# Score tiles in pairs, and the low rotary keys in four strips of 32 rows

## The chip, the cores and the metric

The kernel runs on one core of one Trainium2 chip. TensorE multiplies matrices into PSUM (eight banks of 512 fp32 per partition), VectorE, ScalarE and GpSimd work elementwise, SyncE (SP) issues DMAs. The metric is the time of one execution in device microseconds, lower is better; the median of two runs of the kernel before is 1232.89 us.

## The reference

A two-layer encoder trunk on 1024 tokens of width 1024. Layer 0 projects the normalised input once and feeds two parallel attention groups of eight heads each; layer 1 is windowed attention. The change touches group B of layer 0, multi-head latent attention, whose scores are the sum of a latent part and a rotary part:

```python
def mla_attention(q_lat, q_rope, c_kv, k_rope, w_uv):
    scale = (B_NOPE + B_ROPE) ** -0.5            # 64 + 32 dimensions a head
    def block(args):
        ql, qr = args
        sc = (jnp.einsum('bqhc,bsc->bhqs', ql, c_kv)
              + jnp.einsum('bqhr,bsr->bhqs', qr, k_rope)).astype(jnp.float32) * scale
        p = jax.nn.softmax(sc, axis=-1).astype(c_kv.dtype)
        return jnp.einsum('bhqs,bsc->bqhc', p, c_kv)
    ...
```

The rotary key `k_rope` has 32 dimensions and is shared by all heads; each head has its own 32 rotary query dimensions.

## The kernel before, in words

All large products run in fp32r, and most operands are split into a high part (the value rounded to fp32r) and a low part (the rest), so that a product is the sum of high x high, high x low and low x high.

Layer 0's attention is 32 groups, one for each head and half of the queries: first 16 of group A (names a00 to a71), then 16 of group B (b00 to b71). A group has four score tiles, each of 128 queries by 1024 keys, that is two PSUM banks. For each tile `softmax_unit` (line 1057) issues the score matmuls of the two halves of 512 keys, then a negated row maximum on VectorE (`nm`), the exponential with its row sum on ScalarE (reads PSUM, writes the SBUF tile `P`, `Pa` or `Pb` in the profile), a reciprocal on VectorE (`rs`), and the scaling of `P` on GpSimd. `pv_step` (line 1076) then takes one block of 128 keys: four transposes of `P` into one PSUM bank, a high copy on ScalarE and a low difference on VectorE (`hla`, `hlb`), and two matmuls with the values (`VA`, `VB`) that add into one bank. `run_groups` (line 1097) records, for each group, the eight `pv_step`s of the group before and the four score tiles of this one, the tiles with the priority of the first or second step (`S_AT`).

In group B one half of a score tile is three matmuls with 128 rows (`qk_of`, lines 1343 to 1351): `q1` with `k1` (the latent high keys, and the high rotary key under both the high and the low rotary query), `q2` with `k2` (the latent cross terms), and `q1` with `krl`. `krl` is a 128 x 1024 tile that is zero except for rows 64 to 95, where it holds the low part of the rotary key; those rows meet the high rotary query in rows 64 to 95 of `q1`. It is made once in `b_krope` (line 1218). `b_heads` (line 1310) makes `q1`, `q2`, `k2` for two heads at a time and fetches the rotary rows of `q1` from DRAM (`qr_sp`) by DMAs that GpSimd issues.

The order of the work isn't the order of the program. A `Recorder` (line 106) collects every operation with its tiles, and a list scheduler (`run`) plays them through with a cost for each (`cost`, line 211), eight PSUM banks, 49 SBUF buffers of 4 KB a partition and a window of 400 operations; an operation starts when its engine is free, its inputs are ready and its tiles find room, lowest priority number first. Each engine's queue is then issued in the order so found. All engine instructions carry line 461, where the recorded calls are issued; the tile names tell them apart. An operation made under `issue_after(m)` isn't placed before `m` has started.

Of the kernel before, what the change touches and what calls it, by code (L numbers as in the profile page):

```python
# [19 lines left out]
P = 128  # L20
# [85 lines left out]
class Recorder:  # L106
# [104 lines left out]
    def cost(self, eng, method, regs, kw):  # L211
        n = max(r[4] for r in regs if r[1])
        ps = any(isinstance(r[0], VP) for r in regs)
        nin = max([r[4] for r in regs if not r[1]] or [n])
        if eng == "PE":
            if method == "transpose":
                return 109, 0
            lhs = [r for r in regs if r[0] is kw.get("lhsT")][0]
            c = max(lhs[4] / 1.2, n / 2.4) + 2.5
            if "float32r" not in str(lhs[6].dtype):  # L220
                c = max(426, 4 * n / 2.4 + 3)
            return c, 0
        if eng == "SP":
            return 70, 0
        if method == "dma_start":
            return 1050, 0
        m = max(n, nin)
        if eng == "DVE":
            if method == "reciprocal":
                return 70 + 6.4 * n, 0  # L230
            npt = sum(1 for r in regs if not r[1] and r[4] == 1 and m > 1)
            if method == "tensor_copy":
                return 64 + 1.04 * m if ps else 70 + 0.52 * m, 0
            if method in ("tensor_scalar", "tensor_scalar_mul"):
                return 60 * npt + (67 + 1.04 * m if ps else 70 + 0.52 * m), 0
            return 67 + 1.043 * m + 60 * npt, 0
        if eng == "ACT":
            return (53 if ps else 95) + 0.83 * m + (93 if "bias" in kw or not isinstance(kw.get("scale", 1.0), float) else 0) + (
                93 if "accum_out" in kw else 0), 0
        if method == "tensor_tensor":  # L240
            return (150 + 180 * n, 0) if "pow" in str(kw.get("op")) else (147 + 2.11 * n, 0)
        return 250 + 0.83 * n, 0
# [241 lines left out]
def encoder_kernel(ctx: ExitStack, tc: tile.TileContext, xt, ada_t, w_c1, w_c2, w_c3, w_g0, w_uq, w_ukv, w_out0, w_v1,  # L484
# [30 lines left out]
    def SM(name):  # L515
        return rec.tile(smp, [P, 16], F32, name, "sm")
# [28 lines left out]
    def f(ap):  # L545
        return ap.bitcast(F32)
# [507 lines left out]

    def softmax_unit(qk, name):
        S = PS(f"S{name}")
        first = None
        for b in range(2):  # L1060
            m_ = qk(S[:, b * 512:(b + 1) * 512], b)
            first = first or m_
        marks[name] = first
        nm = SM("nm")
        with rec.at(shift=PRIO["red"]):
            nc.vector.tensor_reduce(out=nm[:, 0:1], in_=S, axis=AX.X, op=ALU.max, negate=True)
        pt = U(f"P{name}")
        sm = SM("sm")
        with rec.at(shift=PRIO["exp"]):
            nc.scalar.activation(pt, S, AF.Exp, bias=nm[:, 0:1], accum_out=sm[:, 0:1])  # L1070
        r = SM("rs")
        nc.vector.reciprocal(r[:, 0:1], sm[:, 0:1])
        nc.gpsimd.tensor_scalar(pt, pt, r[:, 0:1], 1.0, op0=ALU.mult, op1=ALU.mult)
        return pt
# [22 lines left out]
    def run_groups(groups, before, after):  # L1097
        prev = None
        last = {}
        for n in range(len(groups) + 1):  # L1100
            g = groups[n] if n < len(groups) else None
            if g is not None:
                before(n)
                g["P"] = []
            acc = PV(f"pv{prev['name']}") if prev is not None else None
            at = {}
            if prev is not None:
                for kt in range(NT):
                    at[kt] = len(rec.ops)
                    last[n - 1, kt] = pv_step(prev["P"], prev["V"](kt), acc, kt, prev["name"])  # L1110
            if g is not None:
                for j in range(4):
                    with rec.at(at.get(S_AT[j])):
                        g["P"].append(softmax_unit(g["qk"](j), f"{g['name']}{j}"))
            if prev is not None:
                with rec.at(shift=PRIO["fin"]):
                    pv_final(acc, prev["og"](), prev["gate"](), prev["h"], prev["half"])
                prev["done"]()
            if g is not None:
                after(n)  # L1120
            prev = g
# [49 lines left out]
    for h in range(8):  # L1171
        for half in range(2):
            g = h // 4

            def qk_of(j, h=h, half=half, g=g):
                def qk(ps, b):
                    i = half * 4 + j
                    q = Qa[h][:, i * P:(i + 1) * P]
                    m_ = mm(ps, lhsT=q, rhs=khh[g][:, b * 512:(b + 1) * 512], start=True, stop=False)
                    mm(ps, lhsT=q, rhs=kll[g][:, b * 512:(b + 1) * 512], start=False, stop=True)  # L1180
                    return m_
                return qk

            groupsA.append(dict(
                name=f"a{h}{half}", h=h, half=half, qk=qk_of,
                V=lambda kt, g=g: VA[kt // 4][:, kt % 4, g, :, :].rearrange("p s d -> p (s d)"),
                og=lambda p=h // 2: og_get(("0", p)), gate=lambda p=h // 2: gT["0", p],
                done=(lambda p=h // 2: og_done(("0", p), p)) if h % 2 and half else (lambda: None)))
# [29 lines left out]
    def b_krope(mark):  # L1218
        ropeb = U("ropeb")
        load(ropeb[:, 0:512], tabs_d[:, 1024:1536], mark)  # L1220
        load(ropeb[:, 512:768], kr_sp, mark)
        krraw = ropeb[:, 512:768].rearrange("p (t c) -> p t c", t=8)
        rope["C"] = CTv = ropeb[:, 0:256].rearrange("p (t s e) -> p t s e", t=8, s=2)
        rope["S"] = STv = ropeb[:, 256:512].rearrange("p (t s e) -> p t s e", t=8, s=2)
        t = U("krt")
        t1 = t[:, 0:256].rearrange("p (t s e) -> p t s e", t=8, s=2)
        t2 = t[:, 256:512].rearrange("p (t s e) -> p t s e", t=8, s=2)
        z = t[:, 512:768].rearrange("p (t c) -> p t c", t=8)
        kr4 = krraw.rearrange("p t (s e) -> p t s e", s=2)
        nc.gpsimd.tensor_tensor(out=t1, in0=kr4, in1=CTv, op=ALU.mult)  # L1230
        for s in range(2):
            nc.vector.tensor_tensor(out=t2[:, :, s, :], in0=kr4[:, :, 1 - s, :], in1=STv[:, :, s, :], op=ALU.mult)
        nc.vector.tensor_tensor(out=z, in0=t[:, 0:256].rearrange("p (t c) -> p t c", t=8),
                                in1=t[:, 256:512].rearrange("p (t c) -> p t c", t=8), op=ALU.add)
        B["k1"] = [UR(f"k1{j}") for j in range(3)]

        B["krl"] = UR("krl")
        nc.gpsimd.memset(f(B["krl"]), 0.0)
        for half in range(2):
            pt = PT(f"krT{half}")  # L1240
            for j in range(4):
                nc.tensor.transpose(out=pt[0:32, j * P:(j + 1) * P], in_=z[:, half * 4 + j, :], identity=ident)
            c = slice(half * 512, half * 512 + 512)
            k1 = B["k1"][0]
            nc.scalar.copy(k1[64:96, c], pt[0:32, :])
            nc.scalar.copy(k1[96:128, c], pt[0:32, :])
            for other in B["k1"][1:]:
                hi_pool(other[64:128, c], f(k1[64:128, c]))
            sub(B["krl"][64:96, c], pt[0:32, :], f(B["k1"][0][64:96, c]))

    qr_sp = [dr.tile([256, 1024], F32, name=f"qr_sp{s}") for s in range(2)]

# [46 lines left out]
            nc.scalar.copy(vt[:, :, 0, :], v)  # L1299
            sub(vt[:, :, 1, :], v, f(vt[:, :, 0, :]))  # L1300

    q1, q2, k2 = {}, {}, {}

    def K2E(o, i):
        if K2_POOL:
# [4 lines left out]
    def b_heads(p, half):  # L1310
        e, o = 2 * p, 2 * p + 1
        for h in (e, o) if half == 0 else ():
            q1[h], q2[h], k2[h] = UR(f"q1{h}"), UR(f"q2{h}"), UR(f"k2{h}")
            nc.gpsimd.dma_start(out=q1[h][64:96, :], in_=qr_sp[0][h * 32:(h + 1) * 32, :])
            nc.gpsimd.dma_start(out=q1[h][96:128, :], in_=qr_sp[1][h * 32:(h + 1) * 32, :])
        c = slice(half * 512, half * 512 + 512)
        ps = PA(f"kn{p}{half}")
        L = [a[:, p * P:(p + 1) * P] for a in B["ukv"]]
# [22 lines left out]
    for h in range(8):  # L1341
        for half in range(2):
            def qk_of(j, h=h, half=half):
                def qk(ps, b):
                    i = slice((half * 4 + j) * P, (half * 4 + j + 1) * P)
                    s = slice(b * 512, (b + 1) * 512)
                    m_ = mm(ps, lhsT=q1[h][:, i], rhs=B["k1"][h % 3][:, s], start=True, stop=False)
                    mm(ps, lhsT=q2[h][:, i], rhs=k2[h][:, s], start=False, stop=False)
                    mm(ps, lhsT=q1[h][:, i], rhs=B["krl"][:, s], start=False, stop=True)
                    return m_  # L1350
                return qk

            groupsB.append(dict(
                name=f"b{h}{half}", h=h, half=half, qk=qk_of,
                V=lambda kt, h=h: VB[h // 4, kt // 2][:, kt % 2, h % 4, :, :].rearrange("p s d -> p (s d)"),
                og=lambda p=h // 2: og_get(("0", 4 + p)), gate=lambda p=h // 2: gT["0", 4 + p],
                done=(lambda p=h // 2: og_done(("0", 4 + p), 4 + p)) if h % 2 and half else (lambda: None)))
# [449 lines left out]
```

## Time and profile before

| | |
|---|---|
| median of two runs | 1232.89 us (1232.76 to 1233.02) |
| the profiled execution | 1230.13 us, span 1228.4 us |
| mean granted TensorE clock | 0.987 |
| matmuls with `krl` | 128, from 432.1 to 656.8 us |
| score tiles of group B | 64 (64 exponentials into `Pb`) |
| DMA | 106.72 MB, mean 87 GB/s |

The profile is one execution, seen by the hardware profiler. Rows in order of time begin with the start and the duration in us; rows by group end with the count, the busy time in us and the mean duration of one in ns, and behind the second bar the idle time of the engine before them, with what ended it. Rows of one tile give least, median and most in ns and the first and last start. The row of a window gives busy time and count for TensorE, its weight loads, VectorE, ScalarE and GpSimd, then the granted clock, the DMA share and GB/s. `128*128` is the part of the array (rows*columns) that an instruction uses. PE is TensorE, PEld its weight loads, DVE VectorE, ACT ScalarE, POOL GpSimd.

### The profile page before, as it was taken

What the parts mean: (1) busy time and instruction counts of PE and PEld (TensorE: products, weight loads), DVE (VectorE), ACT (ScalarE), POOL (GpSimd) and SP (SyncE); (2) the same over time, 40 slices, a digit from 0 to 9 for tenths busy, and PEclk for the clock granted to TensorE, in tenths of its full rate; (3) what the DMA queues carried; (4) which work ended last, traced back from release to release, by engine and by line L of the source; (5) the groups of instructions that cost most, each with busy time, mean ns of one, the idle gap of its engine ahead of it and who ended that gap; (6) DMA issues with size and microseconds to landing.
All of it is one profiled execution on the core that took longest, in us unless ns stands there. A gap on an engine that the chain in (4) does not pass through costs nothing.

```text
span 1228.4 us, 17931 instructions
## 1 busy us (share of the span) xinstructions
PE 1178.4 (96%) x6320; PEld 987.6 (80%) x6320; DVE 940.8 (77%) x1787; ACT 661.7 (54%) x1348; POOL 566.1 (46%) x551
## 2 busy tenths in 40 slices
PE   7999899999999999999999999899999999998997
PEld 6988788877877877888787888788888778876896
DVE  8977787887787888888889995759875687787243
ACT  4643366566655877787876221338654564653212
POOL 0069754445456545444358223406446354476321
PEclk9999899999999999999999999899999999999999
DMA  9601123131112210101054745000012111055112
GB/s 353 243 9 48 62 76 121 35 120 35 50 59 86 86 52 19 35 17 36 2 202 179 269 157 184 6 18 18 18 52 86 47 58 52 18 188 194 47 70 69
DMA packets 37338, 106.72 MB, mean 87 GB/s; under 512 B 3840, under 2 KB 9472, under 8 KB 37248
## 3 DMA queue, kind: packets, MB, share of 16 engines
q1 hardware_dynamic: 36480, 103.48, 23.9%
q0 software_dynamic: 768, 2.10, 0.7%
q8 instruction: 49, 0.80, 0.3%
q14 instruction: 41, 0.34, 0.1%
HBM read 82.36 MB, written 23.20 MB: 86 GB/s over the span
## 4 chain that ended last, share of the span: by engine, by line
PE 73%; DVE 14%; ACT 4%; issue 3%; POOL 3%; DMA 0%; SPq 0%; POOLq 0%; DVEq 0%; ACTq 0%
PE psum L461 73%; DVE nm L461 3%; DVE p L461 1%; ACT p L461 1%; POOL r L461 1%; DVE xT L461 1%; DVE hla L461 1%; DVE hlb L461 1%; ACT k L461 1%; DVE hl L461 1%; DVE hT01l L461 1%; DVE hT11l L461 1%; DVE q L461 0%; POOL p L461 0%; DVE ada L461 0%
## 5 line engine op out<-in xcount | busy, mean ns | idle before, releaser
L461 DVE TENSOR_REDUCE nm<-psum 128x1 f32<-128x1024 f32 x128 | 155.0, 1218 | 16.1 <-PE psum L461 14.4
L461 POOL TENSOR_SCALAR p<-p,dn 128x384 f32<-128x384 f32 (+1 forms) x128 | 72.9, 589 | 160.5 <-DVE dn L461 118.3
L461 DVE TENSOR_TENSOR hla<-psum,hla 128x512 fp32r<-128x512 f32 x128 | 85.2, 683 | 24.0 <-ACT hla L461 23.2
L461 PE MATMUL psum<-ident,Pa 128*128 128x128 f32 x512 | 94.9, 273 | 1.6 <-POOL Pa L461 1.2
L461 POOL TENSOR_SCALAR Pb<-Pb,rs 128x1024 f32<-128x1024 f32 x64 | 73.0, 1143 | 50.2 <-DVE rs L461 44.6
L461 ACT CAST hla<-psum 128x512 fp32r<-128x512 f32 x128 | 72.9, 592 | 43.0 <-PE psum L461 40.9
L461 PE MATMUL psum<-hla,VA 128*128 128x512 f32 x256 | 94.4, 421 | 1.7 <-DVE hla L461 1.0
L461 POOL TENSOR_SCALAR Pa<-Pa,rs 128x1024 f32<-128x1024 f32 x64 | 74.8, 1173 | 41.1 <-DVE rs L461 35.9
L461 PE MATMUL psum<-hlb,VB 128*128 128x512 f32 x256 | 91.5, 425 | 1.9 <-DVE hlb L461 1.2
L461 ACT ACTIVATE Pa<-psum,nm 128x1024 f32<-128x1024 f32 x64 | 71.7, 1120 | 35.0 <-DVE nm L461 25.5
L461 DVE TENSOR_TENSOR hlb<-psum,hlb 128x512 fp32r<-128x512 f32 x128 | 82.4, 683 | 6.1 <-ACT hlb L461 5.3
L461 ACT ACTIVATE Pb<-psum,nm 128x1024 f32<-128x1024 f32 x64 | 71.8, 1123 | 27.4 <-DVE nm L461 23.0
L461 PE MATMUL psum<-k,q 128*128 128x512 f32 x256 | 83.5, 400 | 0.2 <-ACT Pb L461 0.2
L461 PE MATMUL psum<-ident,Pb 128*128 128x128 f32 x512 | 79.7, 272 | 1.0 <-POOL Pb L461 0.8
L461 DVE CUSTOM_DVE_ANT_0 p<-psum,bias,rows_g 128x384 f32<-128x384 f32 (+1 forms) x128 | 69.9, 579 | 13.0 <-PE psum L461 12.4
L461 ACT ACTIVATE p<-p,nm 128x384 f32<-128x384 f32 (+1 forms) x128 | 74.1, 584 | 7.1 <-DVE nm L461 6.1
L461 PEld LDWEIGHTS psum<-ident,Pa 128*128 128x128 f32 x512 | 65.7, 141 | 14.5 <-POOL Pa L461 1.9
L461 ACT CAST hlb<-psum 128x512 fp32r<-128x512 f32 x128 | 69.2, 602 | 9.4 <-PE psum L461 7.6
L461 PEld LDWEIGHTS psum<-ident,Pb 128*128 128x128 f32 x512 | 63.0, 140 | 12.4 <-POOL Pb L461 1.1
L461 ACT COPY ot<-psum 64x512 f32<-64x512 f32 x64 | 37.4, 584 | 62.2 <-PE psum L461 61.6
L461 PE MATMUL psum<-hl,V 128*128 128x512 f32 x176 | 62.3, 419 | 5.2 <-ACT hl L461 3.5
L461 DVE TENSOR_TENSOR hl<-psum,hl 128x512 fp32r<-128x512 f32 x88 | 55.9, 685 | 10.4 <-ACT hl L461 9.6
(749 smaller groups left out, 3678.3 us busy)
## 6 DMA issues: line engine op xcount, KB each, us to landing
ada<-in_ada_t SPq DMA_DIRECT2D x32, 512.0 KB, 7.1
adag<-in_ada_t SPq DMA_DIRECT2D x16, 512.0 KB, 4.6
o<-spill SPq DMA_DIRECT2D x12, 512.0 KB, 5.7
wo0s<-in_w_out SPq DMA_DIRECT2D x8, 512.0 KB, 8.9
xr<-in_xt SPq DMA_DIRECT2D x8, 512.0 KB, 9.3
x_sp<-xr SPq DMA_DIRECT2D x8, 512.0 KB, 3.0
wo1s<-in_w_out SPq DMA_DIRECT2D x8, 512.0 KB, 5.6
x1r<-x_sp SPq DMA_DIRECT2D x8, 512.0 KB, 3.8
```

The lines of the kernel that those rows point to most:

```text
L461: fn(*[real(v) for v in a], **{k: real(v) for k, v in kw.items()})
```

## The change

Group B's score tiles are made in pairs. For each tile only the two matmuls with 128 rows remain in each half (`q1` x `k1`, `q2` x `k2`). When both tiles of a pair have them, four matmuls with 32 rows follow: strip r (rows 32r to 32r+31) serves tile r // 2 and half r % 2, so that the four write to four different banks. For that the low rotary key stands four times in `krl`, once in each strip, and a new tile `q4` holds the high rotary query of a head four times, fetched from DRAM by one more GpSimd DMA for each head. The first strip is issued behind the last full matmul of the pair, the other three directly behind the first. The maxima and exponentials of both tiles come after that. The scheduler's cost for a matmul with at most 32 rows is set to 127 ns. The zeroing of `krl` is gone, and three GpSimd copies of the first strip into the others come in. Group A goes through the same functions, one tile at a time.

```diff
@@ cost
-            c = max(lhs[4] / 1.2, n / 2.4) + 2.5
+            c = max(lhs[4] / 1.2, n / 2.4) + 2.5 if lhs[5] > 32 else 127
@@ softmax_unit
-    def softmax_unit(qk, name):
+    def scores(qk, name):
         S = PS(f"S{name}")
-        first = None
+        first = last = None
         for b in range(2):
-            m_ = qk(S[:, b * 512:(b + 1) * 512], b)
+            m_, last = qk(S[:, b * 512:(b + 1) * 512], b)
             first = first or m_
         marks[name] = first
+        return S, last
+
+    def softmax_unit(S, name):
         nm = SM("nm")
...
@@ run_groups
-                for j in range(4):
+                n_ = 2 if "low" in g else 1
+                for j in range(0, 4, n_):
                     with rec.at(at.get(S_AT[j])):
-                        g["P"].append(softmax_unit(g["qk"](j), f"{g['name']}{j}"))
+                        S = [scores(g["qk"](j + e), f"{g['name']}{j + e}") for e in range(n_)]
+                        if n_ > 1:
+                            g["low"]([s for s, _ in S], j, mark=S[-1][1])
+                        for e in range(n_):
+                            g["P"].append(softmax_unit(S[e][0], f"{g['name']}{j + e}"))
@@ group A, qk_of
-                    mm(ps, lhsT=q, rhs=kll[g][:, b * 512:(b + 1) * 512], start=False, stop=True)
-                    return m_
+                    return m_, mm(ps, lhsT=q, rhs=kll[g][:, b * 512:(b + 1) * 512], start=False, stop=True)
@@ b_krope
         B["krl"] = UR("krl")
-        nc.gpsimd.memset(f(B["krl"]), 0.0)
...
-            sub(B["krl"][64:96, c], pt[0:32, :], f(B["k1"][0][64:96, c]))
+            sub(B["krl"][0:32, c], pt[0:32, :], f(B["k1"][0][64:96, c]))
+        for r in range(1, 4):
+            hi_pool(B["krl"][32 * r:32 * r + 32, :], f(B["krl"][0:32, :]))
@@ b_heads
+            q4[h] = UR(f"q4{h}")
+            nc.gpsimd.dma_start(out=q4[h], in_=qr_sp[0][h * 32:(h + 1) * 32, :].unsqueeze(0).broadcast_to([4, 32, 1024]))
@@ group B, qk_of
-                    mm(ps, lhsT=q2[h][:, i], rhs=k2[h][:, s], start=False, stop=False)
-                    mm(ps, lhsT=q1[h][:, i], rhs=B["krl"][:, s], start=False, stop=True)
-                    return m_
+                    return m_, mm(ps, lhsT=q2[h][:, i], rhs=k2[h][:, s], start=False, stop=False)
                 return qk
 
+            def low_of(Ss, j, h=h, half=half, mark=None):
+                for r in range(4):
+                    a, b = r // 2, r % 2
+                    i = slice((half * 4 + j + a) * P, (half * 4 + j + a + 1) * P)
+                    with issue_after(mark), rec.at(-1 if r else None):
+                        m_ = mm(Ss[a][:, b * 512:(b + 1) * 512], lhsT=q4[h][32 * r:32 * r + 32, i],
+                                rhs=B["krl"][32 * r:32 * r + 32, b * 512:(b + 1) * 512], start=False, stop=True)
+                    mark = mark if r else m_
+
             groupsB.append(dict(
-                name=f"b{h}{half}", h=h, half=half, qk=qk_of,
+                name=f"b{h}{half}", h=h, half=half, qk=qk_of, low=low_of,
```

More of the change, by code (lines that the diff above doesn't have):

```diff
@@ L1300, in b_values @@
             sub(vt[:, :, 1, :], v, f(vt[:, :, 0, :]))
-    q1, q2, k2 = {}, {}, {}
+    q1, q2, k2, q4 = {}, {}, {}, {}
     def K2E(o, i):
```

## The prediction

> **What bounds the kernel now.** I read the page first (who is busy), then the stretch in which the changed matmuls run, cut out as one window, then its groups by form, its chain, and last the instructions in order of time.
>
> ```profile
> span 1228.4 us, 17931 instructions
> PE 1178.4 (96%) x6320; PEld 987.6 (80%) x6320; DVE 940.8 (77%) x1787; ACT 661.7 (54%) x1348; POOL 566.1 (46%) x551
> L461 PE MATMUL psum<-krl,q x128: 387/392/400, 432.1 to 656.8; 128*128 128x512 f32 x128
> 431.00:657.00 226.00, 222.18 (x1204) 181.04 (x1203) 193.68 (x304) 170.98 (x316) 111.80 (x109) 1.00 0.17 60
> by line: PE psum L461 71.0%; issue 5.9%; DVE nm L461 4.7%; DVE hlb L461 3.6%; ACT k L461 3.1%; ACT Pb L461 2.1%; DVE q L461 2.0%; ACT q L461 1.6%; ACT hlb L461 1.6%; DVE hla L461 0.9%; DVE wo0l L461 0.8%; POOL Pb L461 0.7%; DVE og('0', 7)_1
> ```
>
> The matmuls with the low rotary keys (krl) lie between 432 and 657 us, so group B's scores are a stage of 226 us. There TensorE is busy 222.18, VectorE 193.68 (86%), ScalarE 170.98, GpSimd 111.80, in that order of columns after TensorE's weight loads; the granted clock is 1.00. The chain of waits inside the window puts 71.0% on TensorE. A busy TensorE is not yet one at its peak, so I need what one matmul really occupies.
>
> ```profile
> 500.10 0.61 PE L461 MATMUL psum<-k,q 128*128 128x512 f32 x2
> 500.55 0.39 PE L461 MATMUL psum<-krl,q 128*128 128x512 f32 x1
> 500.78 0.61 PE L461 MATMUL psum<-k,q 128*128 128x512 f32 x2
> 501.23 0.39 PE L461 MATMUL psum<-krl,q 128*128 128x512 f32 x1
> ...
> 524.46 1.58 PE L461 MATMUL psum<-ident,Pb 128*128 128x128 f32 x13
> ...
> L461 PE MATMUL psum<-ident,Pb 128*128 128x128 f32 x463 | 72.7, 272 | 0.1
> L461 PE MATMUL psum<-krl,q 128*128 128x512 f32 x128 | 50.2, 392 | 0.0
> L461 PE MATMUL psum<-ident,Pa 128*128 128x128 f32 x31 | 4.7, 272 | 0.0
> ```
>
> From 500.55 to 501.23 lie three 512-wide matmuls: 0.68 / 3 = 0.227 us from start to start, though one lasts 0.392. Thirteen transposes take 1.58 us, of which the last is 0.272: (1.58 - 0.272) / 12 = 0.109 us each. The window has 1204 matmuls, 463 + 31 of them transposes. So 494 x 0.109 = 53.8 us, and the other 710 at no more than 0.227 = 161.2: up to 215 of 226 us are TensorE's own pace. It is the bound of this stage, with VectorE some 20 us behind it.
>
> **The change part by part.**
>
> *The low product.* 128 full matmuls go, 4 for each pair of tiles: 4 x 0.227 = 0.907 us a pair, 29.1 us in all. In their place come 32 quads of four matmuls with 32 rows each. The trace has no matmul on 32 rows, so I bound a quad from both sides. Cheapest: the four stream side by side, and a quad costs little over one matmul, 0.24 us. Dearest without any extra stall: they stream one after the other, 0.907. Between the two stands the loading of the weights, since each strip still needs its own 128 columns:
>
> ```profile
> 500.33 0.19 PEld L461 LDWEIGHTS psum<-krl,q 128*128 128x128 f32 x1
> 500.56 0.41 PEld L461 LDWEIGHTS psum<-k,q 128*128 128x128 f32 x2
> ...
> 646.41 0.30 PEld L461 LDWEIGHTS psum<-k,q 128*128 128x128 f32 x2
> ...
> L461 PEld LDWEIGHTS psum<-krl,q 128*128 128x128 f32 x128 | 24.0, 188 | 5.4
> ```
>
> The load at 500.33 starts as the matmul before its own starts (500.10 + 0.227) and is over before that one ends: one load ahead, hidden under 512 columns. Where two loads stand together, at 646.41, they take 0.30 us and one takes 0.188: the second follows 0.11 us behind. With the streams side by side, three of the four loads have no stream to hide under, so I take a quad at 3 x 0.11 + 0.227 = 0.557 us. It is the row nearest to the disputed operation, a weight load of the same 128 columns; I assume that it costs no less with 32 rows. Saved: 0.907 - 0.557 = 0.35 us a pair, 32 x 0.35 = 11.2 us of TensorE. The ends are 0 and 32 x (0.907 - 0.24) = 21.3 us.
>
> By the measured 3.07 times for four row tiles of 512 columns that the Trainium skill gives (TensorE: Matmul & The Clock Gate, section Part 3: Packing small matmuls), a quad would be 0.295 us and 19.6 us would go.
>
> *A change of tile shape* could cost more than the quad itself. The nearest rows are transposes that use 32 of the array's columns between others that use 128:
>
> ```profile
> 379.78 0.27 PE L461 MATMUL psum<-ident,krt 128*32 128x128 f32 x1
> 379.89 0.27 PE L461 MATMUL psum<-ident,Pa 128*128 128x128 f32 x1
> 380.00 0.38 PE L461 MATMUL psum<-ident,krt 128*32 128x128 f32 x2
> 380.22 0.49 PE L461 MATMUL psum<-ident,Pa 128*128 128x128 f32 x3
> ```
>
> They follow each other at the same 0.11 us: no stall at either change. That speaks for no cost, but for columns and not for rows. If each change emptied the array, the next start would wait for the end of the last matmul: 0.392 - 0.227 = 0.165 us, twice a quad, 32 x 0.33 = 10.6 us. I take nothing, and keep 10.6 as the other end; a gain is excluded, since no matmul gets shorter. The Trainium skill (TensorEngine Tiling (Array Packing), Key Properties) says that changing the tiling mode drains the array; the rows above do not show it, and the case in which it holds is a rival below.
>
> *The pairing.* Both tiles of a pair are now filled (8 matmuls, 1.82 us) before the quad closes both at 2.37 us; before, they were complete at 1.36 and 2.72. What follows, by these rows:
>
> ```profile
> L461 DVE TENSOR_REDUCE nm<-psum 128x1 f32<-128x1024 f32 x63 | 76.4, 1218 | 7.1 <-PE psum L461 6.0
> L461 ACT ACTIVATE Pb<-psum,nm 128x1024 f32<-128x1024 f32 x63 | 70.7, 1123 | 27.4 <-DVE nm L461 23.0 <-DVE rs L461 3.9 <-POOL Pb L461 0.2
> ...
> 521.49 0.39 PE L461 MATMUL psum<-krl,q 128*128 128x512 f32 x1
> 521.71 0.62 PE L461 MATMUL psum<-k,q 128*128 128x512 f32 x2
> 522.17 0.39 PE L461 MATMUL psum<-krl,q 128*128 128x512 f32 x1
> 522.39 0.62 PE L461 MATMUL psum<-hlb,VB 128*128 128x512 f32 x2
> 522.85 0.38 PE L461 MATMUL psum<-ident,Pb 128*128 128x128 f32 x2
> 522.99 0.71 PE L461 MATMUL psum<-k,q 128*128 128x512 f32 x2
> ...
> 521.48 1.12 ACT L461 ACTIVATE Pb<-psum,nm 128x1024 f32<-128x1024 f32 x1 [1.94 <-DVE nm L461]
> ```
>
> A tile holds two of the eight PSUM banks until its exponential has read it; the transposes and the sum of the group before want two banks or more, so three tiles fit. The trace shows just that: a burst of tiles up to 522.17, then other work, and the fourth tile at 522.99, 0.39 us behind the end of the first exponential (521.48 + 1.12). I count a group's four tiles from its first matmul, with 1.22 for a reduction, 1.12 for an exponential and 0.4 for the two hand-overs. Before: three tiles until 4.09; the first exponential frees its banks at 1.36 + 1.22 + 1.12 + 0.4 = 4.1, and the fourth goes on without a gap. After: the first pair until 2.37, the third tile until 3.28, but the banks for the fourth come at 2.37 + 2.74 = 5.1. For 1.8 us in each group TensorE must live on the group before (8 steps of four transposes and two matmuls: 8 x (4 x 0.109 + 2 x 0.227) = 7.1 us). Uncovered it costs 16 x 1.8 = 29 us, fully covered nothing. Rows 522.39 and 522.85 show such cover in use, so I choose nearly full cover: 2 us of the 29.
>
> *New operands.* Each of 8 heads gets a q4: a GpSimd DMA of 128 rows where q1's moved 32, and one more SBUF buffer. The GpSimd memset of krl goes, and three copies of 32 x 1024 come.
>
> ```profile
> 418.65 2.21 POOL L461 DMA_DIRECT2D q<-qr_sp  x4
> ...
> L461 POOL DMA_DIRECT2D q<-qr_sp x12 | 6.2, 520 | 0.0
> L461 POOL TENSOR_SCALAR Pb<-Pb,rs 128x1024 f32<-128x1024 f32 x62 | 69.8, 1128 | 50.2 <-DVE rs L461 44.6 <-PE psum L461 5.1
> q<-qr_sp POOLq DMA_DIRECT2D x16, 128.0 KB, 2.9
> L461 POOL MEMSET krl<- x1: 961/961/961, 322.4 to 322.4; 128x1024 f32 x1
> ```
>
> An issue is 0.52 us now; with four times the rows it is between 0.52 and 2.1, 4 to 17 us of GpSimd in a stage where it idles 114 of 226 and mostly waits for VectorE's reciprocals (44.6). Queued behind an issue are normalisations of P (Pb) and behind those the transposes. The first use is the tightest: the issues begin at 418.65, the first low product ran at 432.1; two more issues (at most 4.2) and a landing (2.9, perhaps 5 for 512 KB) end by 430.1 (418.65 + 2.21 + 4.2 + 5). The three copies, at no more than 1.13 each (the Pb row has four times the partitions), fall where group A's last heads run, on GpSimd alone. I take nothing; without that cover the first wait would be a few us, once.
>
> *The sum.* The profiled execution took 1230.13 us, its span 1228.4 and 1.7 around it; the median of the runs, 1232.89, is 2.8 above, and I subtract from the median. Not all TensorE time saved is span: 71% of the stage's chain is TensorE's, so 0.71 x 11.2 = 8.0 us, less 2 for the uncovered gap: 6. That gives 1227 us. What is late next is VectorE: its 193.68 us do not shrink, and in a stage of 220 it is 88% busy.
>
> **The rivals.**
>
> *The strips stream and load side by side* (0.24 us a quad): 21.3 us go from TensorE, 0.71 to 1.0 of it from the span, 1212 to 1218; I say 1216. Against it: loads in this trace come one ahead, at 0.11 us. For it: the strips share no rows.
>
> *The gap decides, and it is slower.* Place: the second pair of each group, TensorE waiting for a pair of banks with its fourth tile. Price: up to 29 us against 8 gained. It decides from 8 / 29 = 28% uncovered: then nothing is left. Half uncovered is 14.5 - 8 = 6.5 us slower, about 1240; all of it 1254. For it: banks are full already at 522. Against it: the work of the group before is recorded and ready by then, and TensorE idles little for anything now (1204 matmuls at its pace are 215 of 226).
>
> *It does not overlap, or drains.* The four strips run one after the other: nothing saved, 2 us of gap, 1235. With the drain on both sides 0.71 x 10.6 = 7.5 more: 1242. Against it are the rows at 379.78.
>
> **How the numbers follow.** My forecast, 1227 (1222 to 1231), has a chance of 0.42; side by side 0.18; the gap 0.22; no overlap 0.18, a third of it with drains. The range of 1212 to 1244 takes in the two ends of the quad and half of the gap's ways; outside stay the gap three quarters uncovered or worse and a gain beyond any of these. 2%, about what a measurement of this kernel can tell from no change, is 25 us: the whole of TensorE's possible gain is 21, so faster by more has 0.03, left for a new order of work that is better by chance; slower by more needs the gap wholly uncovered with something beside it, 0.05; within 2% 0.92.
>
> **What the changed profile would show.** Right: low products of 32 rows, in fours, about 0.11 us from start to start, and the next full matmul some 0.56 us after the first of the four; TensorE's chain share falling, the stage about 6 us shorter, the rest of the kernel unchanged. Side by side: starts a few ns apart. Drain: a step of over 0.16 us before the first strip and after the last. The gap: TensorE idle before a tile's first matmul, released by the exponential, some 0.5 us or more a group. Wrong altogether would be a longer wait at the first head of group B for q4, or weight prefetches for the output projection that start later because q4 holds buffers.

## The result, and the profile after

The changed kernel takes 1261.74 us against 1232.89 us: a ratio of 1.0248, 95% interval 1.0214 to 1.0282. It is 29 us slower, where 6 us faster was forecast. The profiled execution's span grew from 1228.4 to 1259.8 us. First the page's head, then the rows of the low product's tile:

```profile
span 1259.8 us, 17961 instructions
PE 1179.6 (94%) x6320; PEld 966.0 (77%) x6320; DVE 946.0 (75%) x1787; ACT 661.4 (53%) x1348; POOL 575.9 (46%) x561
...
L461 PEld LDWEIGHTS psum<-krl,q x128: 181/181/182, 445.7 to 687.6; 32*128 32x128 f32 x128
L461 PE MATMUL psum<-krl,q x128: 488/496/502, 445.7 to 687.6; 32*128 32x512 f32 x128
...
  issue: 11.6, 32
...
L461 PE MATMUL psum<-hlb,VB x256: 387/398/506, 458.8 to 706.9; 128*128 128x512 f32 x128
```

The low products now use 32 rows of the array, as meant. They begin at 445.7 us instead of 432.1 and span 241.9 us instead of 224.7 (656.8 - 432.1): 13.6 + 17.2 = 30.8 us, nearly all of the 31.4 us by which the span grew. The last row is the product with group B's values, which begins at 458.8; it serves below as a mark of the stage.

What TensorE waited for is in the waits of the engine, the stage alone, after the change and then before it (total us, times, longest):

```profile
PE psum L461 <- ACT Pb L461: 23.8, 29, 1.5
PE psum L461 <- DVE hlb L461: 1.2, 3, 0.9
```

```profile
PE psum L461 <- DVE hlb L461: 1.2, 4, 0.5
...
PE psum L461 <- ACT Pb L461: 0.2, 1, 0.2
```

TensorE stood 23.8 us waiting for exponentials, 29 times, where there was one such wait of 0.2 us before. What it did after these waits stands in its groups by tile, in the stage after the change; behind the second bar is the idle time before the group, with what ended it:

```profile
L461 PE MATMUL psum<-hlb,VB 128*128 128x512 f32 x240 | 87.3, 435 | 3.4 <-ACT Pb L461 1.4 <-DVE hlb L461 1.2
L461 PE MATMUL psum<-ident,Pb 128*128 128x128 f32 x482 | 79.0, 274 | 7.2 <-ACT Pb L461 7.1 <-POOL Pb L461 0.2
L461 PE MATMUL psum<-k,q 128*128 128x512 f32 x256 | 76.2, 412 | 14.4 <-ACT Pb L461 14.4
```

14.4 us stood before score matmuls, 7.1 before transposes and 1.4 before products with values: the work of the group before waits for exponentials too. In order of time, from the change's trace, TensorE and its weight loads around one pair, with two rows of VectorE and one of ScalarE:

```profile
513.63 0.27 PE L461 MATMUL psum<-ident,Pb 128*128 128x128 f32 x1
...
518.33 0.49 PE L461 MATMUL psum<-ident,Pb 128*128 128x128 f32 x3
519.00 0.44 PE L461 MATMUL psum<-ident,Pb 128*128 128x128 f32 x2 [0.17 <-POOL Pb L461]
519.98 1.19 PE L461 MATMUL psum<-k,q 128*128 128x512 f32 x4 [0.55 <-ACT Pb L461]
521.10 0.19 PEld L461 LDWEIGHTS psum<-krl,q 32*128 32x128 f32 x4 [0.36 <-issue]
521.10 0.51 PE L461 MATMUL psum<-krl,q 32*128 32x512 f32 x4
521.54 1.07 PEld L461 LDWEIGHTS psum<-ident,Pb 128*128 128x128 f32 x10 [0.25 <-POOL Pb L461]
521.54 1.31 PE L461 MATMUL psum<-ident,Pb 128*128 128x128 f32 x10
521.64 2.35 DVE L461 TENSOR_REDUCE nm<-psum 128x1 f32<-128x1024 f32 x2 [0.38 <-PE psum L461]
522.96 1.11 ACT L461 ACTIVATE Pb<-psum,nm 128x1024 f32<-128x1024 f32 x1
523.91 0.68 DVE L461 TENSOR_TENSOR hlb<-psum,hlb 128x512 fp32r<-128x512 f32 x1
524.21 0.50 PE L461 MATMUL psum<-hlb,VB 128*128 128x512 f32 x1 [1.36 <-ACT Pb L461]
```

The second tile's full matmuls waited 0.55 us for an exponential, ten transposes brought those of the group before to sixteen (1 + 3 + 2 + 10), and then its first product with values waited 1.36 us: it starts 0.14 us after the exponential of 522.96 ends. Sixteen transposes hold four banks, until VectorE has taken their low differences, the first from 523.91 on, behind the two maxima; the pair holds the other four. All eight are taken, and the sum that this product begins needs one. That reading is by count, for the profile doesn't name banks.

### The profile page after: what moved, and what is told of

It reads as the page before. It is cut to its first block, busy times and chain, and to the rows that moved or that the text cites. A ratio compares the mean times of both kernels' runs of the same rounds, so it can differ in the third digit from the quotient of the medians.

```text
span 1259.8 us, 17961 instructions
## 1 busy us (share of the span) xinstructions
PE 1179.6 (94%) x6320; PEld 966.0 (77%) x6320; DVE 946.0 (75%) x1787; ACT 661.4 (53%) x1348; POOL 575.9 (46%) x561
## 3 DMA queue, kind: packets, MB, share of 16 engines
q0 software_dynamic: 4992, 6.31, 2.6%
## 4 chain that ended last, share of the span: by engine, by line
PE 69%; DVE 16%; ACT 6%; issue 4%; POOL 4%; DMA 0%; SPq 0%; POOLq 0%; DVEq 0%; ACTq 0%
PE psum L461 69%; DVE nm L461 4%; ACT Pb L461 2%; DVE p L461 1%; ACT p L461 1%; POOL r L461 1%; DVE hla L461 1%; DVE xT L461 1%; DVE hlb L461 1%; DVE hT11l L461 1%; DVE xr L461 1%; ACT k L461 1%; ACT hlb L461 1%; DVE hT01l L461 1%; DVE qrt L461 1%
## 5 line engine op out<-in xcount | busy, mean ns | idle before, releaser
L461 PE MATMUL psum<-ident,Pb 128*128 128x128 f32 x512 | 83.8, 274 | 10.3 <-ACT Pb L461 7.1
L461 PE MATMUL psum<-k,q 128*128 128x512 f32 x256 | 76.2, 412 | 14.4 <-ACT Pb L461 14.4
L461 PEld LDWEIGHTS psum<-k,q 128*128 128x128 f32 x256 | 44.6, 188 | 31.9 <-ACT Pb L461 20.2
## 6 DMA issues: line engine op xcount, KB each, us to landing
q<-qr_sp POOLq DMA_DIRECT2D x8, 512.0 KB, 11.1
```

The costliest lines, as they stand in the source:

```text
L461: fn(*[real(v) for v in a], **{k: real(v) for k, v in kw.items()})
```

## The experiments

Theory A says that pairing makes tiles hold PSUM banks while they wait for their partner, and TensorE waits for banks that exponentials free. Theory B, its first rival, puts the loss on q4's DMAs and on stalls of the strips themselves. The waits in the table are TensorE's for exponentials; values: first to last product with group B's values.

| run | time, us | ratio to the kernel before | waits, us | values, us |
|---|---|---|---|---|
| before | 1232.89 | | 0.2 | 449.9 to 671.6 |
| the change | 1261.74 | 1.0248 (1.0214 to 1.0282) | 23.8 | 458.8 to 706.9 |
| e1_pair_alone | 1257.17 | 1.0205 (1.0181 to 1.0229) | 19.7 | 456.6 to 698.5 |
| e2_own_rows | 1250.91 | 1.0162 (1.0139 to 1.0185) | 20.8 | 452.7 to 695.7 |
| e3_quad_between | 1249.40 | 1.0144 (1.0119 to 1.0168) | 6.2 | 458.0 to 689.0 |
| e4_plan_cost | 1258.93 | 1.0223 (1.0203 to 1.0244) | 22.1 | 458.6 to 699.3 |
| e5_between_three_dmas | 1238.10 | 1.0056 (1.0040 to 1.0072) | 2.5 | 452.8 to 677.7 |
| e7_pair_three_dmas | 1254.19 | 1.0184 (1.0166 to 1.0202) | 22.2 | 451.0 to 696.3 |
| e8_wide_dmas_alone | 1231.53 | 0.9998 (0.9987 to 1.0009) | 0.6 | 448.1 to 669.5 |
| e9_whole_quads | 1235.72 | 1.0036 (1.0023 to 1.0049) | 8.9 | 450.0 to 675.3 |
| e10_one_strip | 1265.47 | 1.0273 (1.0252 to 1.0294) | 12.7 | 455.1 to 710.2 |
| e11_half_exp_before | 1233.68 | 1.0019 (1.0008 to 1.0029) | none over 0.1 | 451.6 to 674.0 |
| e12_half_exp_after | 1248.18 | 1.0132 (1.0117 to 1.0148) | 10.7 | 459.4 to 689.7 |
| e13_wide_unread | 1261.32 | 1.0251 (1.0224 to 1.0278) | 23.7 | 456.2 to 705.8 |

### The pairing by itself

```diff
-                        m_ = mm(..., lhsT=q4[h][32 * r:32 * r + 32, i],
-                                rhs=B["krl"][32 * r:32 * r + 32, ...], ...)
+                        m_ = mm(..., lhsT=q1[h][:, i], rhs=B["krl"][:, ...], ...)   # krl zero-padded as before, no q4
```

> Only the pairing of the change: both tiles of a pair get their two full matmuls a half, and then the four low products follow as before the change, with 128 rows, q1 and the zero-padded krl. No strips, no q4, no copies of krl, the old cost in the schedule. Theory A (a tile waits for its partner with its PSUM banks held, and TensorE waits for banks that an exponential frees): TensorE's work is that of the kernel before, all of the loss is there and the 11 us of TensorE that the strips saved are not, so 1255 to 1275 us, with TensorE waiting 15 us or more for exponentials in group B (0.2 before, 23.8 with the whole change). Theory B (the loss comes from q4's DMAs at the start of group B and from the strips' own stalls): 1231 to 1238 us and hardly a wait for exponentials.

1257.17 us, 25.0 over the kernel before in the same runs (1232.21), with TensorE's work that of the kernel before. The low products have their old form and pace; only their place is new. TensorE in order of time in this run, and VectorE's next maxima:

```profile
510.26 1.18 PE L461 MATMUL psum<-k,q 128*128 128x512 f32 x4
511.28 0.49 PE L461 MATMUL psum<-ident,Pb 128*128 128x128 f32 x3
513.22 1.20 PE L461 MATMUL psum<-k,q 128*128 128x512 f32 x4 [1.44 <-ACT Pb L461]
514.25 1.08 PE L461 MATMUL psum<-krl,q 128*128 128x512 f32 x4
514.91 2.35 DVE L461 TENSOR_REDUCE nm<-psum 128x1 f32<-128x1024 f32 x2 [0.42 <-PE psum L461]
```

Theory A's mechanism in five rows: the first tile's four full matmuls, three transposes, 1.44 us of nothing until an exponential ends, the second tile, and only then the four low products that let the first tile be read. It sat filled from 511.3 until its maximum began at 514.91. Theory B can't explain this run.

### The change without q4

```diff
-            q4[h] = UR(f"q4{h}")
-            nc.gpsimd.dma_start(out=q4[h], in_=...)
...
-                        m_ = mm(..., lhsT=q4[h][32 * r:32 * r + 32, i],
+                        m_ = mm(..., lhsT=q1[h][32 * r:32 * r + 32, i],
```

> The whole change without q4: the four strips take rows 32r to 32r+31 of q1 as they are, so no DMA and no buffer for q4. Three of four low products then meet other query rows, which leaves the low rotary part of the scores out in its right form; the number, shape and place of the instructions stay. Theory A: q4 costs only the late start, the waits for exponentials stay at 15 us or more: 1248 to 1260 us. Theory B: 1222 to 1236 us, and the first low product near 432 us instead of 445.7.

1250.91 us: 10.8 under the whole change, 6.3 under the pairing alone, and still 20.8 us of waits. So the strips without q4 are faster than the old low products in pairs, leaving q4 out of the change gains too, and neither is the bulk.

### The strips between the two tiles

The edit in short form, with calls abridged:

```diff
-    S = [scores(g["qk"](j + e), ...) for e in range(n_)];  g["low"](both, j, mark=S[-1][1]);  softmax_unit for both
+    S = [scores(g["qk"](j), ...), (PS(...), None)];  g["low"](both, j, mark=S[0][1]);  softmax_unit(S[0][0])
+    scores(g["qk"](j + 1), ..., S[1][0]);  softmax_unit(S[1][0])
```

> The whole change, but the four strips run between the two tiles' full matmuls: the first tile is complete, and its maximum can start, before the second tile's full matmuls. The second tile's banks are taken only for the four strips. Same instructions, same q4. Theory A: the fourth tile of a group gets its banks about 0.9 us earlier (1.45 instead of 2.37 us after the pair began for the first tile), the waits for exponentials fall under 8 us and the time to 1228 to 1243 us. Theory B: no change that matters, 1253 to 1265 us.

The waits for exponentials fell from 23.8 to 6.2 us and the time by 12.3 us, as theory A has it in kind; by the time it stayed over its range (1228 to 1243). Why not more is in TensorE's rows:

```profile
502.77 2.10 PE L461 MATMUL psum<-k,q 128*128 128x512 f32 x8
504.81 0.50 PE L461 MATMUL psum<-krl,q 32*128 32x512 f32 x2
505.24 1.19 PE L461 MATMUL psum<-hlb,VB 128*128 128x512 f32 x4
506.35 0.50 PE L461 MATMUL psum<-krl,q 32*128 32x512 f32 x2
506.79 1.20 PE L461 MATMUL psum<-k,q 128*128 128x512 f32 x4
```

The strips ran two and two in 21 of the 32 quads, because in the plan the second tile's banks were not free at the first two. Two strips take as long as four: 0.43 us to the next start (504.81 to 505.24), as 0.44 for four above. A quad cut in two costs twice.

### The scheduler's cost

```diff
-            c = max(lhs[4] / 1.2, n / 2.4) + 2.5 if lhs[5] > 32 else 127
+            c = max(lhs[4] / 1.2, n / 2.4) + 2.5
```

> The whole change, but the scheduler reckons 216 ns for a strip as for any matmul instead of 127. Only the order of the work can differ. If the loss came from an order laid out for strips that are cheaper than they are (a quad takes some 0.54 us from start to start, the schedule has 0.51), the time would fall towards 1233. Theories A and B both say that it stays between 1255 and 1272 us.

1258.93 us, 2.8 under the change, with 22.1 us of waits. The reckoned cost isn't the cause of the bulk.

### Where q4's share comes from

Three runs. e5 is e3, and e7 the whole change, with q4 fetched by three DMAs of 32 rows instead of one of 128; e8 is the kernel before with the wide DMAs and no reader.

```diff
-            nc.gpsimd.dma_start(out=q4[h], in_=qr_sp[0][h * 32:(h + 1) * 32, :].unsqueeze(0).broadcast_to([4, 32, 1024]))
+            for r in (0, 1, 3):
+                nc.gpsimd.dma_start(out=q4[h][32 * r:32 * r + 32, :], in_=qr_sp[0][h * 32:(h + 1) * 32, :])
...
+    (strip 2 reads q1[h][64:96])
```

> As e3_quad_between, but q4 comes by three DMAs of 32 rows for each head (strips 0, 1 and 3; strip 2 reads q1's own rows 64 to 95) instead of one DMA of 128 rows that repeats 32. Same values. Theory W (the wide DMA is slow: 11 us to land, 528 packets each, and it holds up q1's rows behind it, 8.2 against 2.9 us): e3's 1249.4 falls by about what leaving q4 out gave (10.8), to 1235 to 1243 us. Theory N (the wide DMA is harmless, and leaving it out only gave another order of work): 1246 to 1253 us.

> The whole change in its own order (quad behind both tiles), only with the three narrow DMAs of e5. Theory W: 1247 to 1255 us, as e2_own_rows, and the late start of group B mostly gone (first product with values near 453 us instead of 458.8); the waits for exponentials stay near 20 us (theory A). Theory N: 1257 to 1265 us.

> The kernel before with the change's eight wide DMAs for q4 added at their place, and nothing that reads them: scores, pairing and low products are untouched. Theory W: late q1 rows and GpSimd time delay group B's heads, 1236 to 1245 us. Theory N: 1231 to 1235 us, since no one waits for them.

e5 fell by 11.3 us to 1238.10 and e7 by 7.6 to 1254.19, both inside theory W's ranges. But e8, the DMAs without a reader, cost nothing: 0.9998 (0.9987 to 1.0009). And the wide ones were about as slow there as with the change, by the median time from issue to landing (the last number; 512 KB are q4's, 128 KB q1's), e8 first, then the change:

```profile
q<-qr_sp POOLq DMA_DIRECT2D x8, 512.0 KB, 10.1
q<-qr_sp POOLq DMA_DIRECT2D x16, 128.0 KB, 3.2
```

```profile
q<-qr_sp POOLq DMA_DIRECT2D x8, 512.0 KB, 11.1
q<-qr_sp POOLq DMA_DIRECT2D x16, 128.0 KB, 7.3
```

So slow wide DMAs by themselves cost nothing. q1's rows, though, were late behind them in the change and hardly in e8, so e8 doesn't try that half of theory W. The trace of the change does: no engine waits for a DMA into a q tile anywhere in it; in e8 TensorE did once, 0.7 us. What was left was that the strips wait for q4 in a way that the profile doesn't show, or that the schedule is another one. One more run kept the DMAs and took the reader away:

```diff
                         m_ = mm(...,
-                                lhsT=q4[h][32 * r:32 * r + 32, i],
+                                lhsT=q1[h][32 * r:32 * r + 32, i],
```

> The whole change with its wide DMAs for q4, its order of work and its strips, but the strips read rows 32r to 32r+31 of q1 (as in e2_own_rows), so that nothing waits for q4; the low rotary part of the scores is left out in its right form. e2, without the DMAs, was 10.8 us faster than the whole change, while the DMAs alone cost nothing in e8_wide_dmas_alone. If the difference is the order of work that the scheduler lays out once these DMAs stand in GpSimd's queue: 1257 to 1264 us, as the whole change. If the strips wait for q4 to land: 1248 to 1254, as e2.

1261.32 us, as the whole change, 10.4 over e2. No one waits for q4. By the traces, TensorE, ScalarE, VectorE and GpSimd each go through the same sequence of work as in the change, while in e2 290 of TensorE's 6320 matmuls stand at another place. So what is left, by exclusion, is the order of work that the scheduler lays out with the wide DMAs in GpSimd's queue; it is worse by 10 us. Which step of that order costs it, I didn't isolate: the mark of the first product with values moves from 452.7 (e2) to 456.2, so 3.5 us of it lie ahead of group B's steady part; the values then span 249.6 us instead of 243.0, 6.6 more inside it. The waits for exponentials are 2.9 us longer (23.7 against 20.8).

### Quads that never split

On top of the edits of e5, the first line told in words:

```diff
+    (an operation may claim more tiles than it touches; the first strip claims both score tiles of its pair)
+                    rec.also = () if r else tuple(s.key for s in Ss)
```

> As e5, but the four strips are only issued when the second tile's banks are free, so that they never split into two and two (in e3 most quads did, and half a quad took as long as a whole one, 0.54 us with the step ahead of it); the scheduler reckons 135 ns a strip. The first tile then waits with its banks held, as in the whole change. If splitting is what ate the strips' saving in e3, this is 5 us or more under e5. If holding banks is dearer than splitting (theory A), it is 5 us or more over e5, with more than 10 us of waits for exponentials.

1235.72 us, 2.4 under e5: neither of the two ways by 5. Whole quads save about what the held banks take: the waits rose from 2.5 to 8.9 us. This is the nearest to the kernel before of all that carry the strips, still slower by 0.36% (0.23 to 0.49). I found none that beats the kernel before.

### One strip instead of four

```diff
-                        m_ = mm(..., lhsT=q4[h][32 * r:32 * r + 32, i], rhs=B["krl"][32 * r:32 * r + 32, ...], ...)
+                        m_ = mm(..., lhsT=q1[h][64:96, i], rhs=B["krl"][64:96, ...], ...)
```

> The whole change without q4, and all four low products of a pair in the same strip: rows 64 to 95 of q1 and krl, as they stand there, each with 32 rows. Same values as the reference asks. Theory S (strips stream at the same time because they are different rows of the array, and a visit to them costs a fixed emptying on both sides): the four now follow each other at 0.23 us, a visit takes 0.54 + 3 x 0.227 = 1.2 us, the time is 15 to 22 us over e2_own_rows (1250.9): 1265 to 1273. If a matmul on 32 rows is short in itself, wherever its rows lie: 1248 to 1254.

1265.47 us, 14.6 over e2, as theory S has it at its lower end. TensorE's rows:

```profile
519.57 1.19 PE L461 MATMUL psum<-krl,q 32*128 32x512 f32 x4
520.68 1.31 PE L461 MATMUL psum<-ident,Pb 128*128 128x128 f32 x10
```

The visit takes 1.11 us to the next start against 0.44 with four strips: 0.67 more, 0.22 for each of three matmuls that no longer run beside the first. The order of work is that of e2 in every one of TensorE's 6320 matmuls, so another order isn't what differs. A matmul on 32 rows isn't short; different rows run at once. It also prices TensorE's time in this stage: 32 x 0.67 = 21.4 us of work became 14.6 us of time, 0.68 of it, while the waits for exponentials fell by 8.1 us (20.8 to 12.7): the longer visits filled idle time that the pairing had made.

### Shorter exponentials

```diff
-            nc.scalar.activation(pt, S, AF.Exp, bias=nm[:, 0:1], accum_out=sm[:, 0:1])
+            nc.scalar.activation(pt[:, 0:512], S[:, 0:512], AF.Exp, bias=nm[:, 0:1], accum_out=sm[:, 0:1])
...
+    (GpSimd scales the one half into both)
```

> The kernel before, with a part of group B's softmax left out: the exponential reads only the first 512 keys of a score tile (some 0.5 us shorter) and GpSimd scales it into both halves, by 1 plus the sum instead of a reciprocal. The control for e12_half_exp_after: TensorE waits for exponentials 0.2 us in the kernel before, so the time should hardly move: 1224 to 1233 us.

> The whole change with the same part of group B's softmax left out as in e11. The maxima and their number, the pairing, the strips and q4 stay; only the PSUM banks come free some 0.5 us sooner. Theory A (TensorE waits for banks that exponentials free): the price of the change, 29 us, falls to 10 to 22 us over e11, and TensorE's waits for exponentials by a third or more. Theory L (the loss comes from maxima that come two at a time on VectorE, or from the order of work): the price stays at 25 to 32 us over e11.

The control moved by +0.19% (0.08 to 0.29), a little over its range and not down: the kernel before gains nothing from banks that come free sooner. The changed kernel fell by 13.6 us. The price of the change went from 29 to 14.5 us (1248.18 - 1233.68) and its waits from 23.8 to 10.7. That is theory A; maxima that come in twos on VectorE, theory L, were as many in both and can't be the whole. They may have a part: in the rows at 521.64 and 523.91 above, two maxima in a row hold up the low difference that frees a transposes' bank. And both runs have an order of work of their own (603 of TensorE's 6320 matmuls stand at another place in e11 than in the kernel before, 621 in e12 than in the change), so that the 14.5 us aren't the banks' alone to the last.

## Why the prediction was wrong

**TensorE bounds the stage: right for the kernel before.** e10 turned 0.68 of added TensorE work into time, and the prediction took 0.71. That they agree is luck: 0.71 was a share of the chain before the change, and in e10 the rest filled waits for exponentials (20.8 us without the longer visits, 12.7 with them), of which the kernel before has 0.2 us.

**The quad: right in size, for two wrong reasons that cancel.** Forecast 0.557 us by three weight loads that find no cover. Measured: the last full matmuls ahead of the quad of 521.10 are

```profile
520.55 0.62 PE L461 MATMUL psum<-k,q 128*128 128x512 f32 x2
```

of which the second starts 0.62 - 0.39 = 0.23 us later, at 520.78. From there to the quad are 0.32 us instead of the usual 0.227, and from the quad to what follows 0.44: 0.44 + 0.09 = 0.53 us in all. The medians of all 32 quads are the same, 0.32 and 0.437. But the four loads took 0.19 us together and the four streams 0.51, one matmul's own 0.496 and hardly more: they ran side by side, my first rival. And the changes of rows had a price, which I had held unlikely: the loads stood 0.36 us idle ahead of each quad (11.6 us in 32 times, put down to issue), and the next full load started only with its matmul. Side by side I had at 0.24, so 0.29 is left for the two changes, where I had put 0.33 for a drain on both sides. That the array empties wholly isn't shown: by the trace, in which the ends of matmuls are modelled, the quad starts 0.07 us before the last full matmul ends (519.98 + 1.19 = 521.17). The rows of transposes with 32 columns misled me; what they showed for a change of columns did not hold for a change of rows. There the Trainium skill was nearer (TensorEngine Tiling (Array Packing), Key Properties: changing the tiling mode drains the array), and the trace agrees with it in the loads that stop and the longer steps. The 3.07 times of the Trainium skill's page TensorE: Matmul & The Clock Gate (Part 3) became 0.907 / 0.53 = 1.7 times here, where each quad pays for two changes.

**The saving: about half.** 32 x (0.907 - 0.53) = 12.1 us of TensorE was forecast as 11.2; in time, e2 is 6.3 us under e1, where 0.71 x 11.2 = 8 was forecast. e1 and e2 differ in the order of work too, so 6.3 isn't the strips' alone.

**The pairing: the step that failed.** "So I choose nearly full cover: 2 us of the 29." The runs showed 25.0 us for the pairing alone (e1), and 23.8 us of waits in the change. The price that I had worked out for the gap, up to 29 us, was of the right size; the choice of how much of it is covered was the error. I counted 7.1 us of work of the group before as cover and didn't count that this work needs banks too: its transposes and its sum had to wait for the same exponentials (7.1 and 1.4 us of the 23.8; 524.21 above). The rival with this mechanism had 0.22 and deserved more: the rows at 521.49 to 522.99 already showed three tiles in a burst, and the next tile only behind the end of the first exponential.

**The new operands: a term missed.** DMAs and buffers cost nothing by themselves, as I took it (e8); the three copies were not tried alone. But a schedule that is laid out anew put 10.4 us on top (e13 against e2, by exclusion), and no term of the sum stood for that.

**The sum as it was:** pairing +25.0, strips -6.3, the order of work with q4's DMAs +10.4: +29.1, by e1, e2 and e13. These are steps from run to run, so they add up to e13 by construction; the change showed +28.9. Each step also holds a new order of work, and the 10 us of the last one show how much that can be: the size of a part is less sure than the interval of its run. That the pairing makes the waits is the firm part. The range reached only to half of the gap's ways, 1244, and the true case was the gap nearly whole with something beside it, to which I had given 0.05.

## What to carry to other kernels

Before joining two units of work to save time on the bound engine, count the buffers that the first holds while it waits for the second, and count them for the work that is meant to fill the wait too. Here all eight banks were in use already, and the longer hold was paid nearly in full: 25.0 us of the 29 that it could cost. And a saving that needs another part of the array is worth only what is left after the fixed price of each visit, here 0.53 us for two strips as for four, so few and full visits, or none.

## What the runs showed of the hardware that I had not expected

A visit to the 32-row strips in the middle of full matmuls costs the same for two strips and for four of 512 columns: 0.43 to 0.44 us from its first start to the next full start, with 0.1 ahead. Four weight loads into four strips take 0.19 us together, where two full ones take 0.30. In one strip the matmuls follow each other at about 0.23 us like full ones ((1.19 - 0.50) / 3 in the row at 519.57). GpSimd's DMA that repeats 32 rows four times lands after about 11 us (11.1 in the page of the change) where 32 rows alone took 2.9 in the kernel before, and brought (4992 - 768) / 8 = 528 packets each on its queue. The 32-row DMAs issued among them landed late as well (7.3 us in the change), and in e8 TensorE waited 0.7 us once for a DMA into a q tile.
